# Attention's and the scan's pools each split in two, and a group statistic copied out of its PSUM bank, in a one-layer hybrid encoder step

## The chip, the core and the metric

The kernel runs on one core of one Trainium2 chip. The metric is the device time of one execution in microseconds (us), lower is better. The core has TensorE (matrix products), VectorE, ScalarE, GpSimd and SyncE (SP); here SP issues all the transfers between the device memory and the on-chip memory (SBUF). TensorE writes its results to PSUM, which has eight banks of 2 KB for each of 128 partitions.

## The reference

One layer of an encoder is run over a prompt of 1024 rows and a sample of 64 rows that has a past. Cut to what matters:

```python
xn = _rmsnorm(x, p['norm_mix_w'])
z, xbc, dt_raw, q, k, v, gate_ssm, gate_att = jnp.split(xn @ p['w_in'], ...)
xbc_c, conv_new = _causal_dwconv(conv_past, xbc, ...)          # width 4, then silu
xs, bm, cm = jnp.split(jax.nn.silu(xbc_c), ...)
y_ssm, ssm_new = _ssd_scan(xs, dt, a_neg, bm, cm, ssm_past, chunk_len)
y_ssm = (y_ssm + p['ssm_d'] * xs) * jax.nn.silu(z)
y_ssm = _rmsnorm(y_ssm.reshape(b, t, G, -1), p['ssm_norm_w'])  # over each of 4 groups of 512
o = _diff_attention(rope(rmsnorm(q)), k_all, v_all, q_pos, k_pos, lam)   # softmax pair, a0 - lam * a1
o = _rmsnorm(o, p['subln_w']) * (1.0 - lambda_init)
mix = sigmoid(gate_ssm) * (y_ssm @ p['w_branch_ssm']) + sigmoid(gate_att) * (o @ p['w_branch_attn'])
x = x + mix @ p['w_out']
ha, hb = jnp.split(_rmsnorm(x, p['norm_ffn_w']) @ p['w_up'], 2, axis=-1)
x = x + (jax.nn.silu(_causal_dwconv(ffn_past, ha, ...)) * hb) @ p['w_down']
```

The outputs are x for the prompt and the sample, the keys and values, the scan's states and the last rows of both convolutions.

## The kernel before

Prompt and sample lie side by side as 1088 columns, features on the partitions. The columns are cut in three parts of 384, 384 and 320 (`WIDE`). Each product in float32 is made of three matmuls with operands split in a high and a low half (`product`, L144 to L149); `weights` (L129 to L142) loads a weight block to `w_f` (L139), and ScalarE and VectorE split it (`w_hi` L140, `w_lo` L141).

The work runs in stages:

- Norm, then the v, q and k projections, with rope; the rows go to scratch in the device memory (`q_st`, `k_st`, `c_st`).
- Attention, 8 heads of 9 row blocks. `head_tiles` loads one head's q, k and v; `attend` makes the scores into `sc` (L545, L546), the maximum and exp (L550 or L554, L559), transposes the probabilities into `pt` (L574) and multiplies with v into `po` (L593); `head_out` normalises and stores the head's output (L614 to L621, with the halves `oh` and `ol`).
- The scan, 4 groups by 9 chunks, so 36 steps in 12 spans of `WIDE`. `fetch` loads a span's rows (`in`, `zin`; L654, L656), two spans ahead. `front` makes a step's decay factors from `bc` (L664, L668, L681, L683), transposes x into the bank `tr` (L671) and B into the bank `cb` (L673), copies `cb` out (L676) and forms `xx` (L680). `back` makes the outputs `yi` (L692) and `ye` (L698), and the new state (`stp`, L704 to L711). `gated` multiplies with z and squares; `normed` sums the squares over the group by a matmul with ones into a tile `gst` (L728) that has the tag, and so the bank, of `cb`, takes the inverse root with `rstd_of` (Ln L209, Exp L210, Square L211, two VectorE instructions L212 and L213), scales y (L732) and stores it to `y_sc` (L733).
- The output product, the norm and the feed-forward part.

Between the steps of attention and of the scan, `fill` takes steps of a `filler` on TensorE: the projections of x, z and the gates (`conv_tiles`, `z_tiles`, `gate_tiles`), and later in the scan the first two branch products (`branch`). A filler's result goes to a bank of the pool `pm` (tag `mm`), or, in the scan, to one more bank of the scan's PSUM pool (tag `mx`, through `more` and `acc`).

The order of the instructions on each engine is planned before the run by a scheduler that simulates the times and works by priorities; each engine then runs its own queue in order and waits on semaphores. Memory is handed out in pools. A pool that is opened after another was closed may lie at the same place, and what is written to it waits for the users of the old one. Before the change, attention has one pool in SBUF (`at`) and one in PSUM (`psa`: `sc` with two buffers of two banks, `pt` and `po` with two banks), and the scan has one in SBUF (`sp`) and one in PSUM (`pss`: `tr`, `cb`, `mx`, `yi`, `ye`, `stp`):

```python
    with tc.tile_pool(name="at", bufs=1) as at, tc.tile_pool(name="psa", bufs=1, space=PSUM) as pa:
    ...
    with tc.tile_pool(name="sp", bufs=1) as sp, tc.tile_pool(name="pss", bufs=1, space=PSUM) as pss:
        more = pss, 1
```

Of the kernel before, what the change touches and what calls it, by code (L numbers as in the profile page):

```python
# [17 lines left out]
P = 128  # L18
# [56 lines left out]
def hybrid_layer(ctx: ExitStack, tc: tile.TileContext, xT, prm, cst, rope, wvd, win, wbs, wba, wout, wup, wdn,  # L75
# [409 lines left out]
    with tc.tile_pool(name="at", bufs=1) as at, tc.tile_pool(name="psa", bufs=1, space=PSUM) as pa:  # L485
        lam = at.tile([P, 4], F32, name="lam")
        lt = at.tile([P, 512], F32, name="lt", tag="a_t", bufs=AT)[:, :64]
        wsub = at.tile([P, P], F32, name="wsub")
        V.tensor_scalar_mul(wsub, par[:, O_SUB : O_SUB + P], 1.0 - LAMBDA_INIT)
        for i in range(2):  # L490
            a = O_LAM + 128 * i
            V.tensor_tensor(out=lt, in0=par[:, a : a + 64], in1=par[:, a + 64 : a + 128], op=ALU.mult)
            V.reduce_sum(lam[:, i : i + 1], lt, axis=AX.X)
            act(lam[:, i : i + 1], lam[:, i : i + 1], AF.Exp)
        nlam = at.tile([P, 1], F32, name="nlam")
        V.tensor_tensor(out=nlam, in0=lam[:, 1:2], in1=lam[:, 0:1], op=ALU.subtract)
        V.tensor_scalar_add(nlam, nlam, -LAMBDA_INIT)

        def head_tiles(h):
            def fetch(name, n, b, parts):  # L500
                t = at.tile([P, n], R32, name=name, tag=name, bufs=b)
                for lo, src in parts:
                    load(out=t[lo : lo + src.shape[0]].bitcast(F32), in_=src)
                return t
# [15 lines left out]
        def attend(h, i, tiles, o_t, ssq, s0):  # L520
# [7 lines left out]
            for c in range(2):  # L528
                if nk <= 512:
                    if both is None:  # L530
                        both = pa.tile([P, 1024], F32, name="sc", tag="sc", bufs=2)
# [90 lines left out]

        late = []
        for h in range(8):
            tiles = head_tiles(h)
# [21 lines left out]
    with tc.tile_pool(name="sp", bufs=1) as sp, tc.tile_pool(name="pss", bufs=1, space=PSUM) as pss:  # L647
        more = pss, 1
        def fetch(g, c, w):
            t = sp.tile([P, 6, 384], F32, name="in", tag="in", bufs=2)  # L650
            z = sp.tile([P, 4, 384], F32, name="zin", tag="zin", bufs=2)[:, :, :w]
# [7 lines left out]
        def front(g, ch, o, bx, xs):  # L659
# [3 lines left out]
            bc = sp.tile([P, 8, P], F32, name="bc", tag="bc", bufs=4)  # L663
# [346 lines left out]
```

## Time and profile before

| what | value |
|---|---|
| times of the runs shown, us | 2562.01, 2568.95, 6360.79 |
| their median, us | 2568.95 |
| the profiled execution's own time, us | 2564.99 |
| its span, first to last instruction, us | 2563.2 |
| TensorE busy, us | 2519.5 (98%) |
| VectorE busy, us | 1375.9 (54%) |
| ScalarE busy, us | 1070.6 (42%) |
| GpSimd busy, us | 294.9 (12%) |
| granted TensorE clock, mean | 0.996 |
| bytes moved | 340.42 MB, 133 GB/s in the mean |

Times inside the trace are counted from the span's start. A line of the timeline gives the start, the duration, the engine, the line of the kernel, the operation, out<-in, the shapes and, in brackets, how long the engine had been idle before it and what ended that. SPq is SP's queue: its rows are the issue of transfers, not their duration. `xN` after a row means that N instructions were put together. A wait that has several causes is put down to the one that came last. Matmuls are pipelined, so the busy times of single ones overlap.

### The profile page before, as it was taken

Reading aid. Unit: us, or ns where it says so; the run is one execution under the profiler, and the core shown is the slowest. Engines: PE = TensorE matmul, PEld = TensorE weight load, DVE = VectorE, ACT = ScalarE, POOL = GpSimd, SP = SyncE. Lnnn points to the kernel's source line nnn. Section 1 sums busy time; section 2 is a strip of 40 time slices with the busy share of each in tenths; the row PEclk is TensorE's granted clock in tenths of the full one; section 3 lists DMA queues with packets and bytes.
Section 4 is the critical chain, followed back from the end, with each engine's and each line's share of the span. In section 5 each row is a group of like instructions: output and inputs, shape, how many; then the busy total and the mean of one; then the engine's idle time right before and its main releaser. Section 6 shows DMA issues by size and latency. Waiting matters only on the chain.

```text
span 2563.2 us, 40795 instructions
## 1 busy us (share of the span) xinstructions
PE 2519.5 (98%) x15924; PEld 2436.5 (95%) x15924; DVE 1375.9 (54%) x2359; ACT 1070.6 (42%) x2271; POOL 294.9 (12%) x393
## 2 busy tenths in 40 slices
PE   8999999999999999989999999999999999999999
PEld 8999998999999999988989898999999999999999
DVE  6326265855877577447567657657333333333333
ACT  6234243654666455357455654245313122221221
POOL 3000000100111010014333231022000000000000
PEclk9999999999999999999999999999999999999999
DMA  5218167555445344256796646665311111111112
GB/s 163 82 54 289 47 249 207 164 139 153 119 132 161 112 128 133 68 186 203 219 329 187 226 154 192 193 194 186 120 42 50 42 50 42 43 49 40 44 44 77
DMA packets 216353, 340.42 MB, mean 133 GB/s; under 512 B 28224, under 2 KB 164672, under 8 KB 216032
## 3 DMA queue, kind: packets, MB, share of 16 engines
q1 hardware_dynamic: 216160, 337.81, 42.2%
q8 instruction: 125, 2.05, 0.3%
q14 instruction: 68, 0.56, 0.1%
HBM read 237.60 MB, written 100.13 MB: 132 GB/s over the span
## 4 chain that ended last, share of the span: by engine, by line
PE 86%; DMA 5%; DVE 3%; ACT 3%; SPq 1%; issue 1%; POOL 0%; DVEq 0%; ACTq 0%
PE mm L147 15%; PE mm L149 15%; PE mm L148 15%; PE up L149 7%; PE up L147 7%; PE up L148 7%; PE mx L147 3%; PE mx L149 3%; PE mx L148 3%; PE po L593 3%; PE sc L546 1%; PE sc L545 1%; PE pt L574 1%; DMA b_f<-y_sc 1%; DMA kl_t<-k_st 1%
## 5 line engine op out<-in xcount | busy, mean ns | idle before, releaser
L147 PE MATMUL mm<-xn_hi,w_hi 128*128 128x384 f32 (+1 forms) x1416 | 471.5, 333 | 0.9 <-DVE zr L429 0.9
L149 PE MATMUL mm<-xn_hi,w_lo 128*128 128x384 f32 (+1 forms) x1416 | 468.9, 331 | 0.4 <-DVE w_lo L141 0.4
L148 PE MATMUL mm<-xn_lo,w_hi 128*128 128x384 f32 (+1 forms) x1416 | 467.5, 330 | 0.0
L141 DVE TENSOR_TENSOR w_lo<-w_f,w_hi 128x1024 fp32r<-128x1024 f32 (+2 forms) x196 | 243.5, 1243 | 293.7 <-ACT w_hi L140 293.2
L140 ACT CAST w_hi<-w_f 128x1024 fp32r<-128x1024 f32 (+2 forms) x196 | 203.8, 1041 | 442.8 <-PE mm L148 281.4
L147 PE MATMUL up<-x_hi,w_hi 128*128 128x384 f32 (+1 forms) x1056 | 344.4, 326 | 0.0
L148 PE MATMUL up<-x_lo,w_hi 128*128 128x384 f32 (+1 forms) x1056 | 344.2, 326 | 0.0
L149 PE MATMUL up<-x_hi,w_lo 128*128 128x384 f32 (+1 forms) x1056 | 343.1, 326 | 0.0
L147 PEld LDWEIGHTS mm<-xn_hi,w_hi 128*128 128x128 f32 x1416 | 266.7, 188 | 6.3 <-issue 1.9
L149 PEld LDWEIGHTS mm<-xn_hi,w_lo 128*128 128x128 f32 x1416 | 266.7, 188 | 3.3 <-issue 1.2
L148 PEld LDWEIGHTS mm<-xn_lo,w_hi 128*128 128x128 f32 x1416 | 266.8, 188 | 2.3 <-issue 1.1
L147 PEld LDWEIGHTS up<-x_hi,w_hi 128*128 128x128 f32 x1056 | 198.2, 188 | 0.1
L148 PEld LDWEIGHTS up<-x_lo,w_hi 128*128 128x128 f32 x1056 | 198.2, 188 | 0.0
L149 PEld LDWEIGHTS up<-x_hi,w_lo 128*128 128x128 f32 x1056 | 198.1, 188 | 0.1
L898 DVE TENSOR_TENSOR xa<-xa,mm 128x384 f32<-128x384 f32 x144 | 76.5, 531 | 197.3 <-PE mm L149 197.3
L148 PE MATMUL mm<-f_lo,w_hi 128*128 128x384 f32 (+1 forms) x528 | 173.1, 328 | 0.0
L147 PE MATMUL mm<-f_hi,w_hi 128*128 128x384 f32 (+1 forms) x528 | 173.0, 328 | 0.0
L149 PE MATMUL mm<-f_hi,w_lo 128*128 128x384 f32 (+1 forms) x528 | 173.0, 328 | 0.0
L147 PE MATMUL mm<-b_hi,w_hi 128*128 128x384 f32 (+1 forms) x448 | 149.7, 334 | 3.0 <-DVE b_g L191 2.1
L149 PE MATMUL mm<-b_hi,w_lo 128*128 128x384 f32 (+1 forms) x448 | 146.8, 328 | 2.0 <-DVE w_lo L141 2.0
L148 PE MATMUL mm<-b_lo,w_hi 128*128 128x384 f32 (+1 forms) x448 | 146.6, 327 | 0.0
L458 DVE SCALAR_TENSOR_TENSOR cc<-pre,par,cc 128x384 f32<-128x384 f32 (+1 forms) x216 | 126.5, 586 | 26.0 <-ACT cc L456 20.9
(270 smaller groups left out, 5074.4 us busy)
## 6 DMA issues: line engine op xcount, KB each, us to landing
w_f<-in_win_dram SPq DMA_DIRECT2D x76, 512.0 KB, 4.0
w_f<-in_wup_dram SPq DMA_DIRECT2D x44, 512.0 KB, 3.6
bc<-a_sc SPq DMA_DIRECT2D x32, 512.0 KB, 5.6
w_f<-in_wout_dram SPq DMA_DIRECT2D x24, 512.0 KB, 3.6
x_sc<-cc SPq DMA_DIRECT2D x48, 192.0 KB, 2.0
kh_t<-k_st SPq DMA_DIRECT2D x32, 272.0 KB, 8.4
kl_t<-k_st SPq DMA_DIRECT2D x32, 272.0 KB, 7.8
w_f<-in_wbs_dram SPq DMA_DIRECT2D x16, 512.0 KB, 4.6
```

What stands on the lines that cost most here:

```text
L140: S.copy(hi, w)
L141: V.tensor_tensor(out=lo, in0=w, in1=hi, op=ALU.subtract)
L147: PE.matmul(ps, a_hi, b_hi, start=i == 0, stop=False)
L148: PE.matmul(ps, a_hi, b_lo, start=False, stop=False)
L149: PE.matmul(ps, a_lo, b_hi, start=False, stop=i == n - 1)
L458: V.scalar_tensor_tensor(cc[:, :m], pre[:, i : i + m], cw(i), cc[:, :m], ALU.mult, ALU.add)
L545: PE.matmul(ps[:n, a : a + b], lhs, r_hi, start=True, stop=False)
L546: PE.matmul(ps[:n, a : a + b], lhs, r_lo, start=False, stop=True)
L574: PE.transpose(pt[:kw, (b - b0) * P : (b - b0) * P + n], pr[1][:n, b * P : b * P + kw], ident[:n, :n])
L593: PE.matmul(po[:n, :P], a_t[b // 4][:kw, b % 4 * P : b % 4 * P + n], rhs, start=b == 0, stop=b == nb - 1)
L898: V.tensor_tensor(out=xa[:, m, c : c + w], in0=xa[:, m, c : c + w], in1=ps, op=ALU.add)
```

## The change

- Attention's SBUF pool becomes two: `ak`, opened first, with the tiles of `head_tiles` (q, k, v and the caches), and `at` with the rest. Its PSUM pool becomes `psc` (the `sc` tiles, four banks) and `psa` (`pt`, `po`, two banks).
- The scan's SBUF pool becomes `sin`, opened first, with `in`, `zin` and `bc`, and `sp` with the rest. Its PSUM pool becomes `psi` (`tr`, `cb`, `yi`, `gst` and the fillers' `mx`, four banks) and `pss` (`ye`, `stp`).
- The first head's `head_tiles` is called ahead of the instructions that set up lambda.
- `normed` copies the group sums from `gst` to `rs` in SBUF on ScalarE, and `rstd_of` reads them there.

```diff
-    with tc.tile_pool(name="at", bufs=1) as at, tc.tile_pool(name="psa", bufs=1, space=PSUM) as pa:
-        lam = at.tile([P, 4], F32, name="lam")
...
+    with (tc.tile_pool(name="ak", bufs=1) as ak, tc.tile_pool(name="at", bufs=1) as at,
+          tc.tile_pool(name="psc", bufs=1, space=PSUM) as psc, tc.tile_pool(name="psa", bufs=1, space=PSUM) as pa):
         def head_tiles(h):
             def fetch(name, n, b, parts):
-                t = at.tile([P, n], R32, name=name, tag=name, bufs=b)
+                t = ak.tile([P, n], R32, name=name, tag=name, bufs=b)
...
-            v_t = at.tile([P, 9, P], F32, name="v_t", tag="v_t", bufs=2)
+            v_t = ak.tile([P, 9, P], F32, name="v_t", tag="v_t", bufs=2)
...
-            cv_t = at.tile([P, 4, P], F32, name="cv_t", tag="cv_t", bufs=1)
+            cv_t = ak.tile([P, 4, P], F32, name="cv_t", tag="cv_t", bufs=1)
...
-                    ps = pa.tile([P, 1024], F32, name="sc", tag="sc", bufs=2)
+                    ps = psc.tile([P, 1024], F32, name="sc", tag="sc", bufs=2)
...
+        tiles = head_tiles(0)
+        lam = at.tile([P, 4], F32, name="lam")
...
         for h in range(8):
-            tiles = head_tiles(h)
+            if h:
+                tiles = head_tiles(h)
...
-    with tc.tile_pool(name="sp", bufs=1) as sp, tc.tile_pool(name="pss", bufs=1, space=PSUM) as pss:
-        more = pss, 1
+    with (tc.tile_pool(name="sin", bufs=1) as sin, tc.tile_pool(name="sp", bufs=1) as sp,
+          tc.tile_pool(name="psi", bufs=1, space=PSUM) as psi, tc.tile_pool(name="pss", bufs=1, space=PSUM) as pss):
+        more = psi, 1
         def fetch(g, c, w):
-            t = sp.tile([P, 6, 384], F32, name="in", tag="in", bufs=2)
-            z = sp.tile([P, 4, 384], F32, name="zin", tag="zin", bufs=2)[:, :, :w]
+            t = sin.tile([P, 6, 384], F32, name="in", tag="in", bufs=2)
+            z = sin.tile([P, 4, 384], F32, name="zin", tag="zin", bufs=2)[:, :, :w]
...
-            bc = sp.tile([P, 8, P], F32, name="bc", tag="bc", bufs=4)
+            bc = sin.tile([P, 8, P], F32, name="bc", tag="bc", bufs=4)
...
-            tr = pss.tile([P, 512], F32, name="tr", tag="tr")
+            tr = psi.tile([P, 512], F32, name="tr", tag="tr")
...
-            cb = pss.tile([P, 512], F32, name="cb", tag="cb")
+            cb = psi.tile([P, 512], F32, name="cb", tag="cb")
...
-            yi = pss.tile([P, 4, P], F32, name="yi", tag="yi")
+            yi = psi.tile([P, 4, P], F32, name="yi", tag="yi")
...
-            ps = pss.tile([P, 512], F32, name="gst", tag="cb")[:, :w]
+            ps = psi.tile([P, 512], F32, name="gst", tag="cb")[:, :w]
             PE.matmul(ps, ones, zt[:, 0], start=True, stop=True)
             rs = sp.tile([P, 384], F32, name="grs", tag="grs", bufs=2)[:, :w]
-            rstd_of(sp, rs, ps, w, "gn", 0.25 / 512)
+            S.copy(rs, ps)
+            rstd_of(sp, rs, rs, w, "gn", 0.25 / 512)
```

More of the change, by code (lines that the diff above doesn't have):

```diff
@@ L621, in head_out @@
                     load(out=o_sc[D * u + P * h : D * u + P * (h + 1), b0 * P : b0 * P + w], in_=t.bitcast(F32))
+        tiles = head_tiles(0)
+        lam = at.tile([P, 4], F32, name="lam")
+        lt = at.tile([P, 512], F32, name="lt", tag="a_t", bufs=AT)[:, :64]
+        wsub = at.tile([P, P], F32, name="wsub")
+        V.tensor_scalar_mul(wsub, par[:, O_SUB : O_SUB + P], 1.0 - LAMBDA_INIT)
+        for i in range(2):
+            a = O_LAM + 128 * i
+            V.tensor_tensor(out=lt, in0=par[:, a : a + 64], in1=par[:, a + 64 : a + 128], op=ALU.mult)
+            V.reduce_sum(lam[:, i : i + 1], lt, axis=AX.X)
+            act(lam[:, i : i + 1], lam[:, i : i + 1], AF.Exp)
+        nlam = at.tile([P, 1], F32, name="nlam")
+        V.tensor_tensor(out=nlam, in0=lam[:, 1:2], in1=lam[:, 0:1], op=ALU.subtract)
+        V.tensor_scalar_add(nlam, nlam, -LAMBDA_INIT)
         late = []
         for h in range(8):
-            tiles = head_tiles(h)
+            if h:
+                tiles = head_tiles(h)
             o_t = at.tile([P, 9, P], F32, name="o_t", tag="o_t", bufs=2)
```

13 lines of the change are left out of this document (1 added, 12 removed).

## The prediction

> **What bounds the kernel now.** I read the head of the page first, then the busy time by stages, then the waits of TensorE alone in the scan's stage, and last the order of time round each wait.
>
> ```profile
> PE 2519.5 (98%) x15924; PEld 2436.5 (95%) x15924; DVE 1375.9 (54%) x2359; ACT 1070.6 (42%) x2271; POOL 294.9 (12%) x393
> ```
>
> ```profile
> 0.00:396.00 396.00, 386.48 (x2523) 378.09 (x2524) 181.91 (x308) 155.54 (x319) 23.99 (x37) 1.00 0.44 150
> 396.00:1104.00 708.00, 701.39 (x4484) 674.28 (x4482) 469.89 (x1023) 374.66 (x941) 49.70 (x143) 1.00 0.47 135
> 1104.00:1604.00 500.00, 478.29 (x3157) 433.76 (x3156) 318.96 (x413) 281.37 (x611) 159.44 (x104) 0.98 0.68 216
> 1604.00:2563.20 959.20, 953.34 (x5765) 950.35 (x5764) 405.12 (x617) 259.02 (x401) 61.81 (x109) 1.00 0.26 81
> ```
>
> The columns of the second view are the stretch, its length, the busy time of TensorE, weight load, VectorE, ScalarE and GpSimd, the granted clock, the DMA share and GB/s. TensorE is busy 2519.5 of 2563.2 us, and the change takes no matmul away. So all it can win is idle time (43.7 us in this count) and time at a lowered clock. The third row is the scan: 500.00 − 478.29 = 21.7 us idle, half of the whole, and the only stage whose clock is below 1.00. Attention (second row) idles 6.6 us. The waits of TensorE inside the scan's stage are these:
>
> ```profile
> PE cb L673 <- DVE gn L212: 7.9, 3, 4.7
> PE tr L671 <- DMA in<-x_sc: 4.8, 2, 4.1
> PE mm L147 <- DVE b_g L191: 2.1, 1, 2.1
> PE mx L147 <- DVE ol L619: 1.5, 1, 1.5
> ```
>
> Each row gives us in total, times, longest. Rows one, two and four are what this change is aimed at. The clock falls in the short stretches that hold the longest waits:
>
> ```profile
> 1114.00:1122.00 8.00, 6.21 (x30) 6.18 (x31) 1.75 (x3) 0.37 (x1) 0.00 (x0) 0.79 1.06 375
> 1442.00:1456.00 14.00, 12.61 (x53) 10.67 (x54) 12.92 (x22) 8.72 (x23) 5.38 (x2) 0.63 0.68 214
> 1588.00:1596.00 8.00, 5.94 (x26) 5.70 (x25) 6.44 (x13) 1.34 (x3) 0.00 (x0) 0.79 0.55 182
> ```
>
> At 0.79 over 8 us, 0.21 × 8 = 1.7 us of clock are lost; at 0.63 over 14 us, 0.37 × 14 = 5.2 us.
>
> **Part 1, the boundary from attention to the scan.**
>
> ```profile
> 1091.14 1.05 PE L593 MATMUL po<-v_t,a_t 128*128 128x128 f32 x8
> 1100.45 0.33 SPq L139 DMA_DIRECT2D w_f<-in_win_dram  x1
> 1106.55 0.32 SPq L621 DMA_DIRECT2D o_sc<-ol  x1
> 1106.58 0.44 PE L147 MATMUL mx<-xn_hi,w_hi 128*128 128x384 f32 x1 [1.52 <-DVE ol L619]
> 1108.21 0.80 SPq L654 DMA_DIRECT2D in<-x_sc  x2
> 1109.05 6.70 DMA in<-x_sc
> 1110.90 1.05 ACT L140 CAST w_hi<-w_f 128x1024 fp32r<-128x1024 f32 x1 [5.06 <-PE mx L148]
> 1113.00 0.56 SPq L656 DMA_DIRECT2D zin<-z_sc  x1
> 1115.79 0.90 PE L671 MATMUL tr<-con,in 128*128 128x128 f32 x4 [4.14 <-DMA in<-x_sc]
> ```
>
> The scan's first load (L654) is issued only after the last store of attention's output (L621) has gone, and the filler's bank `mx` opens only when VectorE has read the last `pt` bank (L619). Those are the last users of attention's pools, though `in` and `mx` need only their own place: I read it as one wait for the whole old pool. With two pools, `in`, `zin` and `bc` lie over the q, k and v tiles, whose last reader is the `po` matmul that ends at 1092.2. The four `psi` banks lie over the `sc` banks. The loads can then go some 14 us earlier (to about 1094), land after 6.7 us at about 1101, and be there when TensorE now idles at 1105 and 1111. Removed: 1.52 + 4.14 = 5.7 us, and the 1.7 us of clock behind them: 7.4 us at most, 0 at least if the loads don't move.
>
> What follows next? `e2`, `b_cb` and `xx` stay in a pool that overlaps the end of attention's memory, so ScalarE's and VectorE's part of the first step still waits for about 1108. The first steps also show two short waits (the last row here is a transfer's: how often, KB, us to landing):
>
> ```profile
> 1137.65 0.44 PE L147 MATMUL mx<-xn_hi,w_hi 128*128 128x384 f32 x1 [0.80 <-DVE zr L429]
> 1163.64 0.63 PE L671 MATMUL tr<-con,in 128*128 128x128 f32 x4 [0.66 <-DMA in<-x_sc]
> ...
> w_f<-in_win_dram SPq DMA_DIRECT2D x76, 512.0 KB, 4.0
> ```
>
> I keep their sum, 1.5 us, as the price of an early start whose other operands are not ready. On SP the fetches are issued between 1108.21 and 1113.56, 5.4 us; moved ahead, they stand before the weight load of 1100.45 (landing 4.0 us after issue) and the output stores. 1100.45 + 5.4 + 4.0 = 1109.9, and its cast starts at 1110.90: covered by 1 us, and up to 5.4 us late if the fetch also crowds the engines, whose share is 1.06 in the first stretch above. I take 0 of that and keep 5.4 for the range. **Boundary: −7.4 + 1.5 = −5.9 us** (from −7.4 to +5.4).
>
> **Part 2, the statistics copied out of their bank.**
>
> ```profile
> 1199.38 1.28 ACT L209 ACT_TABLE_LOAD   x1
> 1205.60 0.33 PE L673 MATMUL cb<-con,in 128*128 128x128 f32 x1 [1.25 <-DVE gn L212]
> 1278.92 1.28 ACT L209 ACT_TABLE_LOAD   x1
> 1283.84 0.33 PE L673 MATMUL cb<-con,in 128*128 128x128 f32 x1 [1.88 <-DVE gn L212]
> 1424.64 0.88 PE L728 MATMUL gst<-zin,con 128*128 128x384 f32 x2 [0.47 <-ACT b_cb L676]
> 1435.43 1.28 ACT L209 ACT_TABLE_LOAD   x1
> 1442.79 0.55 DVE L212 SCALAR_TENSOR_TENSOR gn<-gst,gn 128x384 f32<-128x384 f32 x1
> 1443.39 0.33 PE L673 MATMUL cb<-con,in 128*128 128x128 f32 x1 [4.74 <-DVE gn L212]
> ```
>
> `gst` shares the one `cb` bank with the transposes of the next step, and holds it until L212 has read it, behind Ln with a table load, Exp, and Square on ScalarE. A copy at the place of the first table load frees the bank instead. Its price is the nearest row of like shape:
>
> ```profile
> L187 ACT COPY b_g<-mm 128x384 f32<-128x384 f32 (+1 forms) x16 | 7.1, 443 | 9.5 <-PE mm L149 9.5
> ```
>
> With 0.44 us the bank is free at 1199.8, 1279.4 and 1435.9. TensorE came to it at 1205.60 − 1.25 = 1204.35, at 1281.96 and at 1438.65: no wait is left, by 4.5, 2.6 and 2.8 us. Removed: 7.9 us. The clock's 5.2 us at 1442 to 1456 follow the longest of them and should go too. **Bank: −13.1 us** (from −13.1 to −7.9 if the clock falls all the same).
>
> The Trainium skill, "TensorE: Matmul & The Clock Gate", section "Part 1: The HAM clock gate (the warmup mystery)", has the clock halved after an idle window of about 3.4 us. By that rule the waits of 4.14 and 4.74 us trip it and the short ones do not, so all 6.9 us return; the rows differ in one place, since the clock also fell at 1588, after a wait of 2.06 us, so a short leftover could keep part of it.
>
> The copies themselves: 12 × 0.443 = 5.3 us on ScalarE, which is busy 281 of 500 us in the stage. They lengthen each normalisation by 0.44 us. That is hidden by filler matmuls, except where the chain ends on TensorE:
>
> ```profile
> 1582.30 1.28 ACT L209 ACT_TABLE_LOAD   x1
> 1587.85 1.94 DVE L732 SCALAR_TENSOR_TENSOR y<-y,par,grs 128x320 f32<-128x320 f32 x4
> 1590.31 0.54 PE L147 MATMUL mm<-b_hi,w_hi 128*128 128x384 f32 x1 [2.06 <-DVE b_g L191]
> ```
>
> Here b_g L191 stands behind L732 on VectorE and TensorE waits for it. I charge this place and one more (the y rows that the first branch over y_sc loads): **+0.9 us**, from 0.4 to 5.3.
>
> The Trainium skill, "VectorE: DVE Perf Modes", section "Rules for kernel authors", speaks against the copy: take operands from PSUM as they are, or copy first only for many operations. Here two readers follow, so by that rule the copies are 5.3 us lost and the sum would be 4.4 us higher, 2551. The sum above goes by the waits on the bank instead: what the copy buys is the bank and not a faster read.
>
> **Part 3, the first head's loads ahead of the lambda set-up, and attention's two pools.** TensorE's first scores wait for a load of k, not for the set-up:
>
> ```profile
> 396.42 1.51 SPq L503 DMA_DIRECT2D q_t<-q_st  x3
> 399.11 0.15 DVE L497 TENSOR_SCALAR nlam<-nlam 128x1 f32<-128x1 f32 x1
> 414.81 0.47 PE L546 MATMUL sc<-kl_t,q_t 128*128 128x512 f32 x1 [1.14 <-DMA kl_t<-k_st]
> ```
>
> The set-up ends at 399.1, 15 us before the scores run, and both halves of the memory still follow the same q/k stage. 0 us; at most 1.1 either way.
>
> **The sum.** The profiled execution took 2564.99 us around a span of 2563.2. It lies between the two closest of the runs shown, 2562.01 and 2568.95 (their median). 2565.0 − 5.9 − 13.1 + 0.9 = **2546.9 us**, 0.7% under the profiled execution and 0.9% under the median. Best case: 2565.0 − 7.4 − 13.1 + 0.4 = 2544.9, and runs lie up to 3 us under the profiled one: 2542. With a leftover clock dip and the copies exposed the forecast's own range is 2542 to 2556.
>
> **Rivals.**
>
> *The gain is given back at the scan's end.* From 1563 to 1590 the chain of waits runs over loads of y_sc, ScalarE and VectorE, with TensorE idle in small pieces. If that chain doesn't move up, TensorE reaches it earlier and waits longer. Then part 2 is lost and the boundary stays: 2565.0 − 5.9 + 0.9 = 2560. For it: the 2.1 us row. Against it: TensorE paces the 36 scan steps through matmuls in one queue, so the chain should come earlier with them.
>
> *The split does not do what it says:* the loads are held by something else, such as SP's queue. Part 1 is 0: 2565.0 − 13.1 + 0.9 = 2553. Against it: L654 goes out 1.7 us after the last L621.
>
> *Slower: the freed bank draws the next transposes ahead of ScalarE.* The order on TensorE is planned beforehand. If the planner takes the copy as done at once, it puts the `cb` transposes straight behind `gst`, ahead of filler matmuls, and TensorE stands until ScalarE, in order, reaches the copy. That ScalarE is late shows at 1424.64 + 0.88 = 1425.5 against 1435.43. At the mean of the three waits, 7.9 / 3 = 2.6 us, plus 0.44, at all 12 places: 36.5 us for the 7.9 there now, and no clock regained: 2565.0 − 5.9 − 7.9 + 36.5 = 2588. It decides once the 12 together pass 7.9 + 5.2 + 5.9 = 19 us, 1.6 us each. Spread to all 36 steps that use this bank it is 36 × 3.04 = 109 us and 2661. Against both: fillers have stood between in all but three cases.
>
> **Chances.** Forecast 0.52; given back 0.17; split idle 0.10; slower at the 12 places 0.12; slower at all steps, or another loss of that size, 0.07; something faster by over 2% 0.02, since 2% is 51 us and only 43.7 us of idle time and the 8.6 us of clock in the three rows above are there to be won. Faster and slower by over 2%, about what a measurement of this kernel can tell from no change, have 0.02 and 0.07; the rest, 0.91, is within 2%. The range reaches from 2541 (one us under the best case) to the slower rival at 2588.
>
> **What would show it.** Right: the first L654 is issued before 1097, no `tr` wait of 4 us, no `mx` wait on L619; no wait of `cb` on L212, 12 new ScalarE copies of about 0.44 us; the clock 1.00 round the eighth `gst`; scan stage near 482 us. Wrong: L654 still behind the last L621; a wait of `cb` on the new copy of over 1.6 us in the mean; the wait on b_g L191, or those on y_sc loads, grown by 10 us; TensorE's busy time changed by more than 5 us, which would mean that the order changed elsewhere.

## The result and the profile after

| kernel | median us (runs) | ratio to before, 95% interval |
|---|---|---|
| before | 2565.36 (2561.38 to 2569.66, and one of 6360.79; 10 runs) | 1 |
| changed | 2558.16 (2555.86 to 2559.6, 10 runs) | 0.9972 [0.9963, 0.9981] |

The change gains 7.2 us, 0.28%; the ratio leaves out the one execution of 6360.79 us. The forecast was 2546.9, so 11 us of the gain are missing. The profiled execution of the changed kernel took 2559.57 us around a span of 2557.7.

The first row of the changed kernel's page with the busy times, and then its windows by stage (columns as in the prediction): the scan's stage first, then four shorter stretches:

```profile
PE 2521.8 (99%) x15924; PEld 2439.8 (95%) x15924; DVE 1378.1 (54%) x2359; ACT 1074.6 (42%) x2283; POOL 292.8 (11%) x393
```

```profile
1104.00:1604.00 500.00, 483.76 (x3175) 439.18 (x3174) 325.11 (x419) 286.09 (x624) 159.29 (x104) 0.98 0.67 212
...
1194.00:1206.00 12.00, 11.29 (x37) 9.33 (x38) 4.04 (x8) 9.00 (x20) 1.09 (x1) 0.57 0.62 190
1428.00:1458.00 30.00, 26.79 (x157) 23.47 (x158) 19.74 (x30) 23.70 (x57) 8.62 (x5) 0.89 0.78 247
1566.00:1596.00 30.00, 26.48 (x138) 25.77 (x138) 17.83 (x33) 13.15 (x23) 3.29 (x2) 0.89 0.75 244
...
1090.00:1190.00 100.00, 98.65 (x682) 89.74 (x681) 59.04 (x82) 63.52 (x148) 35.86 (x25) 1.00 0.63 204
```

The twelve copies show as ScalarE's 2283 instructions for 2271. TensorE has the same work and 500.00 − 483.76 = 16.2 us of idle time in the scan, where it had 21.7. The clock did not come back: at 1194 it is 0.57 over 12 us, 5.2 us lost at a place where the kernel before lost none. The rows at 1428 and 1566 lose 0.11 × 30 = 3.3 us each. That is 11.8 us of clock in the scan; the three rows of the prediction have 8.6 for the kernel before.

TensorE's waits in the scan's stage now (total, times, longest, us):

```profile
PE mm L147 <- ACT b_hi L171: 5.3, 3, 2.7
PE cb L677 <- ACT grs L734: 4.3, 2, 2.8
...
PE ye L702 <- DVE y L703: 1.2, 1, 1.2
```

The waits of `tr` on its load and of `mx` on attention's last bank are gone. The wait of `cb` on L212 is gone by name, and a wait of the same instruction on the new copy (L734) stands in its place. New are 5.3 us on the casts of rows of `y_sc` (`b_hi`, L171).

The timeline at the boundary from attention to the scan:

```profile
1089.54 1.05 PE L581 MATMUL po<-v_t,a_t 128*128 128x128 f32 x8
1090.63 0.79 SPq L658 DMA_DIRECT2D in<-x_sc  x2
...
1096.36 10.06 SPq L668 DMA_DIRECT2D bc<-a_sc  x4
...
1098.24 0.27 PE L675 MATMUL tr<-con,in 128*128 128x128 f32 x1
...
1108.47 0.38 SPq L609 DMA_DIRECT2D o_sc<-oh  x1
```

The first load goes out with the end of the last `po` matmul, 17.6 us earlier than before (1108.21), and `tr` runs at 1098 without a wait.

And the timeline at two of the copies, the places of the waits of 1.5 and 2.8 us:

```profile
1187.14 0.81 PE L732 MATMUL gst<-zin,con 128*128 128x384 f32 x2
...
1190.10 4.20 ACT L687 ACTIVATE bc<-bc,nacum 128x128 f32<-128x128 f32 x14
1194.20 0.46 ACT L734 COPY grs<-gst 128x384 f32<-128x384 f32 x1
...
1194.71 0.33 PE L677 MATMUL cb<-con,in 128*128 128x128 f32 x1 [1.53 <-ACT grs L734]
...
1418.26 0.88 PE L732 MATMUL gst<-zin,con 128*128 128x384 f32 x2 [1.30 <-ACT b_cb L680]
...
1426.23 2.44 ACT L687 ACTIVATE bc<-bc,nacum 128x128 f32<-128x128 f32 x8
1428.58 0.45 ACT L734 COPY grs<-gst 128x384 f32<-128x384 f32 x1
...
1429.09 0.33 PE L677 MATMUL cb<-con,in 128*128 128x128 f32 x1 [2.76 <-ACT grs L734]
```

`gst` is done at 1187.95 and at 1419.14; the copies start 6.2 and 9.4 us later, because other work stands ahead of them in ScalarE's queue. TensorE has come to `cb` by then, and earlier than it would without the copies. The fillers are counted by the matmuls into `mm` and `mx`: in the two traces, 19 to 24 filler matmuls stand between a `gst` and the next `cb` at the first ten places, and 24 to 48 with the pools alone (e3 below; 22 and 48 behind the eighth, at 1418).

### The profile page after: what moved, and what is told of

It is laid out like the page before. It is cut to its first block, busy times and chain, and to the rows that moved or that the text cites. A ratio compares the mean times of both kernels' runs of the same rounds, so it can differ in the third digit from the quotient of the medians.

```text
span 2557.7 us, 40802 instructions
## 1 busy us (share of the span) xinstructions
PE 2521.8 (99%) x15924; PEld 2439.8 (95%) x15924; DVE 1378.1 (54%) x2359; ACT 1074.6 (42%) x2283; POOL 292.8 (11%) x393
## 4 chain that ended last, share of the span: by engine, by line
PE 71%; DMA 4%; ACT 3%; DVE 3%; issue 1%; SPq 0%; POOL 0%; DVEq 0%; ACTq 0%; POOLq 0%
PE mm L147 13%; PE mm L149 13%; PE mm L148 12%; PE up L149 7%; PE up L147 7%; PE up L148 7%; PE po L581 3%; DMA b_f<-y_sc 1%; PE sc L534 1%; PE sc L533 1%; PE pt L562 1%; PE mx L149 1%; PE mx L147 1%; PE mx L148 1%; PE yi L696 1%
```

## The experiments

Each kernel was timed in five rounds beside the kernel before on the same chip, those of one letter together. Medians in us; across letters the ratios are compared, a difference of 0.001 being 2.6 us.

| run | what it is | us | ratio to before |
|---|---|---|---|
| e1 | the changed kernel again | 2558.42 | 0.9971 [0.9959, 0.9982] |
| e2 | copies only | 2565.53 | 0.9996 [0.9985, 1.0006] |
| e3 | pools only | 2552.94 | 0.9948 [0.9935, 0.9961] |
| e4 | both, copies on VectorE | 2556.85 | 0.9962 [0.9948, 0.9976] |
| f1 | PSUM pools only | 2554.42 | 0.9950 [0.9938, 0.9962] |
| f2 | SBUF pools only | 2569.44 | 1.0014 [1.0005, 1.0023] |
| f3 | both, bank still held | 2559.45 | 0.9971 [0.9961, 0.9982] |
| f4 | pools, `gst` in the bank of `stp`, no copy | 2562.96 | 0.9991 [0.9982, 0.9999] |
| g1 | changed, one cast moved off ScalarE | 2563.18 | 0.9987 [0.9978, 0.9997] |
| g2 | pools, copy in the last normalisation only | 2557.15 | 0.9956 [0.9942, 0.9969] |
| g3 | pools, copies not in the last group | 2556.94 | 0.9959 [0.9945, 0.9973] |
| g4 | pools, copy in the eighth normalisation only | 2553.21 | 0.9945 [0.9930, 0.9960] |
| h1 | pools, copies off every chain | 2554.91 | 0.9957 [0.9945, 0.9970] |
| h2 | pools, last chain longer | 2555.45 | 0.9962 [0.9948, 0.9975] |
| h3 | pools, fewer fillers in the scan | 2541.47 | 0.9908 [0.9894, 0.9921] |
| i1 | before, fewer fillers | 2563.01 | 0.9994 [0.9985, 1.0003] |
| i2 | changed, fewer fillers | 2556.32 | 0.9968 [0.9957, 0.9980] |
| i3 | pools, still fewer fillers | 2563.45 | 0.9995 [0.9985, 1.0005] |

Most intervals are 0.0025 wide, some 6 us, so two kernels of the table that lie 3 us apart are not told apart by it.

### Which part of the change does what (e1 to e4)

e1 has no edit. e2 is the kernel before with the copy, e3 the changed kernel without it, e4 the copy on another engine:

```diff
 e2, on before:
+            S.copy(rs, ps)
-            rstd_of(sp, rs, ps, w, "gn", 0.25 / 512)
+            rstd_of(sp, rs, rs, w, "gn", 0.25 / 512)
 e3, on the changed kernel:
-            S.copy(rs, ps)
-            rstd_of(sp, rs, rs, w, "gn", 0.25 / 512)
+            rstd_of(sp, rs, ps, w, "gn", 0.25 / 512)
 e4, on the changed kernel:
-            S.copy(rs, ps)
+            V.tensor_copy(rs, ps)
```

> The changed kernel as it is, once more. Its first profile shows TensorE at half clock five times in the scan (10.24 us from 1195, then 3.4 us at 1430, 1454, 1567 and 1591: 23.9 us, 11.9 us lost; before: 17.1 us, 8.5 us lost). Theory 'the dips belong to the program': the same five dips within a few us, mean clock 0.995 to 0.996, 2558 us. Rival 'the dips fall by chance, as the clock's windows happen to lie to the waits': the waits of TensorE are the same within 1 us, but dips come at other places or with other lengths, and mean clock and time move together by 2 to 5 us.

> The kernel before with the copy of the group sums alone; all pools as before. The forecast's theory (the bank is free 0.44 us after the place of the table load): no wait of cb on the statistics, clock not below 1.00 round the eighth group sum, 12 us faster than before, 2553 us. Rival 'ScalarE is late, and the plan puts the copy behind the exps of bc': the copy starts 5 to 10 us after its matmul at two or three of the twelve places, cb still waits 3 to 5 us in all where it waited 7.9, and the gain is 2 to 5 us, 2560 to 2563 us.

> The changed kernel without the copy: the pools alone. The forecast's theory: no wait at the boundary on attention's last store, 6 us faster than before, 2559 us, and cb still waits about 8 us on L212. Rival 'the boundary's gain is spent in the next 100 us (new waits and a clock dip at 1195)': the boundary's waits are gone, but only 2 to 4 us are left at the scan's end, 2561 to 2563 us. If the two parts simply add, this run and the copy alone together are 7.2 us faster than before.

> The changed kernel with the copy on VectorE in place of ScalarE. Theory 'ScalarE's queue makes the copy late': VectorE is free or nearly so at both places where cb waits on the copy (group sums at 1187 and 1418), so the copy ends within 2.5 us of the matmul, the 4.3 us of waits on it go, and with them a clock dip of 1.7 to 5.1 us: 3 to 9 us faster than the changed kernel, 2549 to 2555 us. Rival 'what is freed at the bank is lost elsewhere (loads of y_sc, the next wait)': the waits on the copy go, others grow, and the time stays within 2 us of 2558; the twelve copies of 0.53 us on VectorE cost up to 6 us more.

The pools alone win 13.1 us. The copies alone win nothing, and on top of the pools they cost 5.5 us (e3 to e1, 2558.42 − 2552.94). So the missing 11 us all lie with the copies, and the pools bring more than forecast (e3 is faster than both of its expectations). The two parts do not add: alone they gain 13.1 and 0.5 us, together 7.6 (e1, on the same chip).

In e1's trace the clock falls at the same five places as in the first trace of this kernel, the first time for 6.8 us instead of 10.2, and its ten executions reach from 2552.1 to 2562.0. So the places recur and the lengths vary, and each of its two expectations is right in a part. e2 has neither of its times: `cb` still waits 3.0 us, on the copy, as the rival said, but next to nothing is gained. With the copies on VectorE (e4) the kernel is not told apart from either; the waits on the copy are gone and others have come up (`gst` 3.3 us on the copy of `b_cb`, `ye` 2.1 us), as e4's rival has it.

TensorE's waits in the scan with the pools alone:

```profile
PE cb L677 <- DVE gn L212: 6.3, 3, 4.9
PE yi L696 <- DVE bc L688: 2.5, 1, 2.5
PE mm L147 <- DVE b_g L191: 1.8, 1, 1.8
```

The bank's waits are still there (6.3 us), and no cast of `y_sc` is waited for. The copies trade 6.3 us on L212 for 4.3 on L734 and 5.3 on L171.

### Which pool is the lock (f1, f2)

f1 takes the split of the SBUF pools back, f2 that of the PSUM pools; neither has a copy.

```diff
 f1:
-    with (tc.tile_pool(name="sin", bufs=1) as sin, tc.tile_pool(name="sp", bufs=1) as sp,
+    with (tc.tile_pool(name="sp", bufs=1) as sp,
 f2:
-          tc.tile_pool(name="psi", bufs=1, space=PSUM) as psi, tc.tile_pool(name="pss", bufs=1, space=PSUM) as pss):
-        more = psi, 1
+          tc.tile_pool(name="pss", bufs=1, space=PSUM) as pss):
+        more = pss, 1
```

> Only the PSUM pools are split (psc/psa, psi/pss); memory stays one pool each, and there is no copy. Theory (the boundary is paid by two locks, memory and banks, each with its own price): the wait of mx on L619 (1.5 us before) goes, the wait of tr on the load of in stays at 4 us or a little more, because L654's load still follows the last store L621; time 1 to 3 us under before, about 2564 where before is 2566. Rival (the locks act only together, the later one sets the end): no change within 1 us, 2566. Rival (banks are the main lock): 9 us or more under before, about 2556.

> Only the memory pools are split (ak/at, sin/sp); PSUM stays one pool each, and there is no copy. Theory (two locks): the loads of the first scan step are issued some 14 us earlier than before and the 4.1 us wait of tr on them goes; mx and tr still open only when VectorE has read the last pt bank (L619 of before), so a wait of about 1.5 us stays; with the clock of that place 5 to 7 us under before, about 2560. Rival (the locks act only together): no change, 2566. Rival (memory is all of it): 13 us under before, 2553, like both splits together.

For f1 the rival with the banks as the main lock holds; f2 lies above all three of its expected times. The window from 1090 to 1190 in the kernel before, in f1 and in f2:

```profile
1090.00:1190.00 100.00, 91.92 (x617) 83.31 (x616) 57.33 (x78) 59.22 (x139) 33.63 (x22) 0.98 0.62 196
```

```profile
1090.00:1190.00 100.00, 97.56 (x675) 88.88 (x675) 58.23 (x79) 60.86 (x144) 32.84 (x24) 1.00 0.64 202
```

```profile
1090.00:1190.00 100.00, 85.20 (x577) 77.63 (x576) 55.82 (x76) 58.20 (x137) 31.87 (x21) 0.93 0.60 191
```

In the same 100 us TensorE runs 617, 675 and 577 matmuls. In f1 the first load is issued as late as before:

```profile
1108.78 0.80 SPq L658 DMA_DIRECT2D in<-x_sc  x2
```

Yet TensorE idles for only 2.4 us in its window, since the fillers' bank `mx` is free and the plan puts more fillers between the last `po` and the first `tr`, 131 instead of 97. In f2 the loads are early and it goes worse; its timeline:

```profile
1089.93 1.53 SPq L658 DMA_DIRECT2D in<-x_sc  x2
...
1095.48 10.24 SPq L668 DMA_DIRECT2D bc<-a_sc  x4
...
1107.79 0.88 SPq L609 DMA_DIRECT2D o_sc<-oh  x2
...
1114.15 0.23 DVE L607 TENSOR_TENSOR ol<-pt,oh 128x64 fp32r<-128x64 f32 x1 [14.41 <-DMA o_sc<-oh]
...
1114.43 1.11 PE L675 MATMUL tr<-con,in 128*128 128x128 f32 x4 [11.65 <-DVE ol L607]
```

The `bc` loads stand in SP's queue for 10 us, attention's last stores wait behind them, L606 and L607 wait for the stores, and `tr` waits 11.65 us, since the scan's one bank pool opens only when attention's last `pt` bank has been read. In the changed kernel the stores are as late (1108.47, above), but `tr` no longer needs those banks. So the SBUF split is harmful by itself. Whether it adds anything to the PSUM split (e3 under f1 by 1.5 us) is not told.

### Why the copies cost: the bank, the time or the order (f3, f4, g1)

f3 makes the copies but reads on from the bank, so that it stays held. f4 makes none and puts `gst` in another bank. g1 is the changed kernel with one cast of L171 per branch on GpSimd.

```diff
 f3, on the changed kernel (the copy is read by nobody):
-            rstd_of(sp, rs, rs, w, "gn", 0.25 / 512)
+            rstd_of(sp, rs, ps, w, "gn", 0.25 / 512)
 f4, on e3:
-            ps = psi.tile([P, 512], F32, name="gst", tag="cb")[:, :w]
+            ps = pss.tile([P, 512], F32, name="gst", tag="stp")[:, :w]
 g1, on the changed kernel:
-                    S.copy(hi[:, k], t)
+                    (G.tensor_copy if (c, k) == (768, 3) else S.copy)(hi[:, k], t)
```

> Both pool splits, and the twelve ScalarE copies are made, but L212 goes on reading the bank, which therefore stays held; the copied tile is read by nobody. Theory 1 (the copies lose on top of the pools because they free the bank, and the order on TensorE then takes the cb transposes ahead of fillers and stands behind a late ScalarE): the loss goes with the freed bank, time within 1.5 us of the 2552.9 of the pools alone. Theory 2 (the copies' own 12 x 0.44 us on ScalarE, in front of casts that TensorE waits for, are the loss): 5 us above the pools alone, about 2558, as in the changed kernel, with the waits of mm on b_hi at the end of the scan.

> Both pool splits and no copy; the statistics gst stand in the bank of stp instead of cb, so that the cb transposes never wait for the normalisation, and the next stp (which comes 3 to 20 matmuls after the transposes) does. Theory 1 (what is lost is the early order behind a late ScalarE, not the ScalarE time of a copy): the 4.9 us wait of cb on L212 goes, but stp, later in its step, waits in its place for the same reader, shorter by the work between: 0 to 4 us under the pools alone, 2549 to 2553. Theory 2 (only the ScalarE time of the copies hurt, and a free cb bank is worth its whole 6.3 us of waits and the clock behind): 9 us or more under the pools alone, 2544 or less.

> The changed kernel, in which one y_sc cast of each of the two branches that read y_sc (column block 768, row block 3; L171) is made on GpSimd instead of ScalarE. The orders on TensorE and VectorE are the changed kernel's; on ScalarE the last copy L734 then stands behind three casts, as the last Ln does with the pools alone, and not behind a fourth one that waits for its y_sc load until 1575.7. Theory 1 (at the scan's end the changed kernel pays for the order on ScalarE, not for the copy): the last normalisation starts about 3 us earlier and the wait of mm on b_hi at 1588 (2.8 us) falls under 1 us; 2.5 to 4 us under the changed kernel, 2554 to 2556. Theory 2 (the copies' own 12 x 0.44 us on the chain): no change, 2558 to 2559.

f3 costs some 6 us over the pools alone (0.9971 to 0.9948) with the bank still held and with 24 to 48 fillers behind a `gst`, as without the copies, so my theory that the freed bank is the harm falls. f4 frees the bank of `cb` with no copy at all and is 11 us slower than the pools alone (0.9991), which neither of its expectations had. Its waits:

```profile
PE stp L708 <- DVE gn L212: 8.7, 6, 2.8
PE cb L677 <- ACT b_cb L680: 5.5, 2, 4.8
PE mm L147 <- ACT b_hi L171: 4.0, 2, 2.5
```

The same reader L212 is waited for, only in another bank, and more in sum; so f4 does not show what a free bank is worth. g1 was to mend ScalarE's order at the scan's end, and both of its expectations missed: it is 4 us slower than the changed kernel (0.9987 to 0.9971 and 0.9972). There the copy no longer stands behind the cast but behind TensorE itself:

```profile
1578.87 0.43 ACT L734 COPY grs<-gst 128x320 f32<-128x320 f32 x1 [2.63 <-PE gst L732]
```

So at the scan's end the last `gst` is late on TensorE. (Where g1's own 4 us lie is not shown: from the last `stp` to the first `mix` matmul it takes 114.4 us, the changed kernel 114.6.) In the planned orders 90 filler matmuls stand between the last `stp` and it wherever every normalisation has a ScalarE copy (the changed kernel, e2, f3, g1), and 74 in the kernel before, e3, e4, f1 and g2 to g4; f4, without a copy, has 96. At 0.15 to 0.17 us each, the distance of fillers' starts in the timeline, 16 are 2.4 to 2.8 us. In the traces the last `gst` starts 19.0 us after the end of the last `stp` in the changed kernel and 14.6 in e3.

### One copy at a time (g2 to g4)

```diff
 on e3, with the condition (g, c) == (3, 768) for g2, g < 3 for g3, (g, c) == (2, 384) for g4:
-            rstd_of(sp, rs, ps, w, "gn", 0.25 / 512)
+            src = ps
+            if <condition>:
+                S.copy(rs, ps)
+                src = rs
+            rstd_of(sp, rs, src, w, "gn", 0.25 / 512)
```

> Both pool splits, and the copy in the last of the twelve normalisations only; in this kernel's order it stands behind three casts, as the last Ln does with the pools alone. Theory 1 (order, not copy): the chain at the scan's end is longer by the copy's 0.44 us at most; 2553 to 2554, within 1 us of the pools alone (2552.9). Theory 2 (a copy on this chain is what costs the 3 us at the scan's end): 2556 or more.

> Both pool splits, and the copy in the nine normalisations of the first three groups, not in the last group's three; the order on ScalarE at the scan's end is that of the pools alone (three casts ahead of the last Ln). Theory 1: the 3 to 5 us that the changed kernel loses after 1550 are not there, what it loses at 1180 to 1205 (about 4 us) and gains at 1427 to 1454 (about 2 us) stays: 2554 to 2556. Theory 2 (each copy costs about the same, 5.5 us over twelve): 2557 to 2558.

> Both pool splits, and the copy in one normalisation only, the eighth, where cb waits 4.9 us for L212 with the pools alone and the clock is halved for 13.7 us behind it (6.8 us lost). If a copy in time frees the bank there, up to 11.7 us are to be had; the copy stands on ScalarE behind the first eight L687 and y_sc casts, as in the changed kernel, where cb still waited 2.8 us there. Theory 1 (the bank is free only when ScalarE gets to the copy): 2 to 6 us under the pools alone, 2547 to 2551, with a cb wait on the copy of 1 to 3 us and a half-clock stretch of 3.4 us. Rival (the bank is what holds TensorE, and one copy frees it): 9 us or more, 2544 or less. Rival (the wait only moves to another operand that ScalarE makes): 2552 or more.

g2, one copy in the last normalisation, is 2 us over the pools alone by the ratio (0.9956 to 0.9948) and 4 by the median: it goes with the theory that a copy on this chain costs, and its trace says the same (below). g3, with the nine copies of the first three groups, lies between its two expectations, 3 us over the pools alone, and its interval takes in both. g4 stands level with e3, as the last of its three expectations has it. In its trace `cb` waits 3.1 us at 1427 instead of 4.9, and then two casts of L171 are waited for, 1.8 us, with a dip of the clock of their own: the rival in which the wait moves to another product of ScalarE.

### Time, or length of the last chain (h1, h2)

```diff
 h1, on e3:
+            S.copy(rs, con[:, :w])
             rstd_of(sp, rs, ps, w, "gn", 0.25 / 512)
 h2, on e3 (copies read by nobody):
+            for _ in range(6 if (g, c) == (3, 768) else 0):
+                S.copy(rs, ps)
             rstd_of(sp, rs, ps, w, "gn", 0.25 / 512)
```

> Both pool splits; in each of the twelve normalisations ScalarE copies a constant tile into grs ahead of its use (0.42 to 0.47 us each, the same size as the changed kernel's copies). The copy needs no result of gst, so it lies on no chain, frees no bank, and the order at the scan's end is that of the pools alone (74 filler matmuls ahead of the last gst). Theory 1 (the copies cost by standing between gst and Ln, on the chain to the y_sc casts): within 2 us of the pools alone, 2551 to 2555, and no new wait of mm on b_hi over 1.5 us after 1560. Theory 2 (12 x 0.44 us more ScalarE work is the cost, wherever it stands): 5 us over the pools alone, 2558.

> Both pool splits; in the last normalisation alone ScalarE copies gst six times into a tile that is not read, ahead of Ln, so that this one chain is about 2.5 us longer; the bank stays held and the order on TensorE ahead of the last gst is that of the pools alone (74 fillers). Theory 1 (the y_sc round trip behind the last normalisation sets the scan's end, with next to no slack): from the last stp to the y_sc casts 34 us instead of 31.4, from the last stp to the first mix matmul 113 to 114 us instead of 110.7, a wait of mm on b_hi of 2 to 4 us near 1585; time 2 to 4 us over the pools alone, 2555 to 2557. Theory 2 (that chain has cover): the 2.5 us lie beside fillers, no wait on b_hi grows, 2552 to 2553.5.

h1 has the copies' ScalarE time without their place on a chain. It is 2 us over e3, within the intervals of both, and its scan ends as with the pools alone, so the theory that twelve copies' time is the price wherever they stand gets less than half of its 5 us. h2 lengthens one chain. By tile, the last `stp` and the first matmuls of the output product (a row gives the count, the shortest, middle and longest ns, the first and last start) in e3, in the changed kernel and in h2:

```profile
L708 PE MATMUL stp<-xx,b_cb x2: 589/641/693, 1553.1 to 1553.6; 64*128 64x512 f32 x2
...
L147 PE MATMUL mm<-mix,w_hi x30: 336/336/338, 1664.8 to 1680.0; 128*128 128x384 f32 x30
```

```profile
L708 PE MATMUL stp<-xx,b_cb x2: 589/641/693, 1555.1 to 1555.6; 64*128 64x512 f32 x2
...
L147 PE MATMUL mm<-mix,w_hi x19: 336/336/368, 1670.2 to 1679.6; 128*128 128x384 f32 x19
```

```profile
L708 PE MATMUL stp<-xx,b_cb x2: 589/641/693, 1551.2 to 1551.7; 64*128 64x512 f32 x2
...
L147 PE MATMUL mm<-mix,w_hi x26: 336/336/416, 1666.4 to 1679.6; 128*128 128x384 f32 x26
```

And the timelines of the same three, ScalarE's first casts of `y_sc` rows that follow the last normalisation, in h2 with the matmul that waits for them:

```profile
1585.56 1.35 ACT L171 CAST b_hi<-b_f 128x320 fp32r<-128x320 f32 x3 [1.77 <-DMA b_f<-y_sc]
```

```profile
1590.75 0.88 ACT L171 CAST b_hi<-b_f 128x320 fp32r<-128x320 f32 x2 [1.24 <-DMA b_f<-y_sc]
```

```profile
1586.80 0.89 ACT L171 CAST b_hi<-b_f 128x320 fp32r<-128x320 f32 x2 [1.22 <-DMA b_f<-y_sc]
...
1587.31 0.56 PE L147 MATMUL mm<-b_hi,w_hi 128*128 128x320 f32 x2 [2.72 <-ACT b_hi L171]
```

From the last start of `stp` to the first `mix` matmul it is 111.2 us in e3, 114.6 in the changed kernel and 114.7 in h2; and to the casts 32.0, 35.1 and 35.1. (Taken from the end of `stp`, 110.2 to 111.2 us in the kernel before, e3, f1, f2, g3, g4 and h1, whose last normalisation has no copy; 113.1 to 115.4 in the changed kernel, e1, e2, e4, f3, g1, g2 and h2, which all have copies in it; and 117.3 in f4, which has none, but 96 fillers ahead of the last `gst`.) The store and load of `y_sc` behind the last normalisation set the scan's end with next to no slack, and h2's 2.5 us come back as 3.5. Of the copies' 5.5 us, 3.4 lie here. The later `gst` (19.0 us behind `stp` instead of 14.6) is enough for it. What a copy costs here by itself is less clear: g2's single copy takes 0.42 us, and its stretch is 2.5 us longer than e3's (113.7 instead of 111.2), of which I cannot place 2.

### With more fillers left for the scan's end (h3, i1 to i3)

```diff
-SCAN_STEPS = 1.65
+SCAN_STEPS = 1.5     # h3 on e3, i1 on before, i2 on the changed kernel; 1.4 for i3 on e3
```

> Both pool splits without the copies, and fewer filler matmuls in the scan (SCAN_STEPS 1.5 instead of 1.65), so that more of them are left to lie beside the y_sc round trip at its end. If the waits at the scan's end (1.1 and 1.8 us and a half-clock stretch of 3.4 us with the pools alone) are a lack of filler there, they go: 2 to 4 us under the pools alone, 2549 to 2551. If the scan's own steps need the fillers as cover, waits of yi and cb inside the scan grow by more than that: 2555 or more.

> The kernel before, with SCAN_STEPS 1.5 instead of 1.65 and nothing else; no split, no copy. If the gain of fewer fillers in the scan (11 us on top of the pools) and that of the pools (13 us) are separate, this stands 10 to 12 us under before, 2553 to 2556. If the fewer fillers only pay because the pools moved the boundary, within 3 us of before, 2562 to 2568.

> The changed kernel with SCAN_STEPS 1.5 instead of 1.65: both splits and the twelve copies. Theory 1 (with 1.65 the copies cost because they make the y_sc round trip at the scan's end later, where no filler covers it): with the round trip covered by the fillers that are left over, the copies cost nothing or gain the cb waits that are left with the pools at this setting (4.4 us): 2537 to 2543, against 2541.5 without the copies. Theory 2 (the copies cost inside the scan, through the order that they give TensorE and ScalarE): 4 us or more above it, 2545.5 or more.

> Both pool splits without the copies, SCAN_STEPS 1.4: one more step in the direction that won 11 us. If filler at the scan's end is still short at 1.5, 2 us or more faster, 2539.5 or less; at 1.5 no wait of over 0.9 us is left after 1445, so I expect nothing there and more waits in the scan's steps for want of cover: 2541 to 2547.

h3 beats both kernels: 24 us under before, 10 under the pools alone (0.9908 to 0.9948). The same setting does nothing without the split (i1), and with the copies it brings 1 us, which is not told from nothing (i2, 0.9968 to 0.9972). At 1.4 all is lost again (i3), so 1.5 is one order that fits and no trend; neither h3 nor i3 came out at one of its expected times. i3's executions reach from 2553.0 to 2566.5 us with granted clocks from 0.997 down to 0.993, and the one with the trace is the fastest, so the trace does not show its loss. TensorE's waits in the scan in h3, and its window from 1424 to 1470:

```profile
PE cb L677 <- DVE gn L212: 4.4, 2, 3.3
PE yi L696 <- DVE bc L688: 3.9, 2, 2.4
```

```profile
1424.00:1470.00 46.00, 42.60 (x285) 38.17 (x284) 35.24 (x46) 28.48 (x65) 16.34 (x10) 0.96 0.77 242
```

At 0.96 over 46 us, 1.8 us of clock are lost. With the pools alone at 1.65 it is 0.34 × 20 = 6.8 us at this place, and 1.8 more in the window from 1566 to 1596 (0.94), where h3 stands at 1.00:

```profile
1426.00:1446.00 20.00, 15.09 (x68) 12.74 (x67) 12.41 (x24) 13.74 (x36) 6.24 (x2) 0.66 0.71 219
```

So over half of what the rate brings is clock: some 7 us of the 10 to 11.

The same of i2, with the copies:

```profile
PE mm L147 <- ACT b_hi L171: 3.2, 1, 3.2
PE mm L148 <- DVE b_lo L172: 2.8, 1, 2.8
PE yi L696 <- ACT y L706: 2.6, 1, 2.6
PE mx L147 <- ACT w_hi L140: 2.5, 1, 2.5
...
PE cb L677 <- ACT grs L734: 1.7, 2, 1.6
```

```profile
1424.00:1470.00 46.00, 36.55 (x206) 32.19 (x205) 32.99 (x45) 28.69 (x65) 13.63 (x10) 0.89 0.66 207
```

The copies do what they are for, 4.4 us of waits for the bank fall to 1.7, and TensorE waits instead for casts, copies and weights that the same ScalarE makes, or VectorE right behind it (`b_lo`): 206 matmuls in 46 us instead of 285. This falls inside the scan and not at its end, so at this rate my theory that the loss is the end's alone falls.

### Where the time lies, in two stretches

The scan can be cut at three matmuls: the end of the last `po`, the last start of `stp`, and the first matmul with `mix`. In the kernel before the first is at 1092.19 (in the prediction) and the second at 1564.3; in e3 they are at 1090.00 and 1553.6 (above):

```profile
L704 PE MATMUL stp<-xx,b_cb x4: 589/594/693, 1552.2 to 1564.3; 128*128 128x512 f32 x2, 64*128 64x512 f32 x2
```

```profile
1088.95 1.05 PE L581 MATMUL po<-v_t,a_t 128*128 128x128 f32 x8
```

| trace | last `po` to last `stp`, us | last `stp` to first `mix`, us |
|---|---|---|
| before | 472.1 | 111.3 |
| e2, copies only | 465.4 | 116.0 |
| e3, pools only | 463.6 | 111.2 |
| changed | 465.0 | 114.6 |
| e1, changed again | 463.1 | 115.0 |
| h3, pools at 1.5 | 429.1 | 134.1 |
| i2, changed at 1.5 | 441.8 | 136.9 |

Each row is one execution, and the two of the changed kernel differ by 1.9 us in the first stretch. There the pools gain 8.5 us and the copies alone 6.7, but both together only 7.1 and 9.0: the two gains overlap, and on top of the pools the copies bring nothing. In the second stretch every row with copies is longer: by 3.4 to 4.7 us at 1.65, by 2.8 at 1.5. At 1.5 the copies cost 12.7 us in the first stretch as well.

## Why the prediction was wrong

**Part 1, the boundary: right in what goes, wrong in why, and too small.** The signs named came true: the first load before 1097, no wait of `tr` and of `mx`. The step that failed is "The loads can then go some 14 us earlier ... and be there when TensorE now idles". The earlier loads alone bring nothing (f2); the four banks bring it (f1). The size, −5.9, was too small by the 1.5 us that I kept for two short waits, which did not stay: from 1090 to 1190 TensorE was idle for 100 − 91.92 = 8.1 us before, for 2.5 us in e3 and for 1.35 us in the changed kernel. That is 5.6 to 6.7 us, and with the 1.7 us of clock 7.3 to 8.4. The traces agree: 8.5 us up to the last `stp`. The pools' times measure 13.1. Of the rest the two traces show 2.2 us ahead of the last `po` (1092.2 to 1090.0), 1.7 of it a fall of the clock near 437 us that of the two only the trace of the kernel before has; and the two profiled executions lie some 2 us nearer together than the medians. The 5.4 us that I kept for loads ahead of the stores in SP's queue were real: they are f2's mechanism, at 11.65 us. In the changed kernel the stores are as late, and TensorE does not wait for them.

**Part 2, the copies: wrong.** The forecast was −13.1 for the bank and +0.9 for the copies; on top of the pools they measure +5.5. The first failed step is "A copy at the place of the first table load frees the bank ... no wait is left". I held TensorE's order fixed; the plan made it anew and put `cb` up to 26 fillers nearer to `gst`, while the copies started 6.2 and 9.4 us after it, and 4.3 us of 7.9 stayed. That ScalarE is late stood in the slower rival with its row, and the sum did not use it. The second is "Removed: 7.9 us" as a gain on top of part 1: in g4, e4 and i2 a wait taken from the bank comes back as a wait for what ScalarE and VectorE make next, and the gains of the two parts overlap. Of the bank's −13.1 on top of the boundary nothing was had: from the last `po` to the last `stp` the copies add 1.4 us to e3 in one execution and take 0.5 in the other (e1). The third is the clock, "should go too": it fell at 1194 behind waits of 1.2 and 1.5 us, and the scan lost 11.8 us to it instead of 8.6. The copies' price of 0.9 left out the chain at the scan's end, which costs 3.4 us. The sign that I named for a changed order, TensorE's busy time, did not show it: it moved by 2.3 us while the fillers between `gst` and `cb` went from between 24 and 54 to between 19 and 24.

The Trainium skill, "VectorE: DVE Perf Modes", section "Rules for kernel authors", advises to copy out of PSUM first only for many operations. The trace agrees in the sign (e3 against e1, 5.5 us), though the runs show another reason than the copies' time: in h1 that time is not told from nothing.

**Part 3** cost nothing that the traces show.

**The sum.** Part 1 was 13.1 instead of 5.9, the copies +5.5 instead of −12.2: 7.2 us better and 17.7 worse, 2546.9 − 7.2 + 17.7 = 2557.4, against 2558.2.

**The rivals.** "The gain is given back at the scan's end" (2560) came nearest and names the right chain, loads of `y_sc`, ScalarE and VectorE. For the copies alone it fits: e2 gains 6.7 us inside the scan and gives back 4.7 at its end. With the pools it holds for 3.4 us, and there is no gain of the copies to give back; that its 2560 lies so near 2558.2 is in part luck, since two errors offset each other: its boundary was too small (5.9 for 13.1), and so was its price of the copies (0.9 for 5.5). "The freed bank draws the next transposes ahead of ScalarE" is what the plan did, at all of the first ten places, but TensorE stood at two only, 4.3 us in sum, under the 19 us from which it would decide: 19 or more fillers were left between. That the split would do nothing is refuted by e3.

**Open:** why the plan gives up cover with twelve copies that it keeps without them, why the gains of the pools and of the copies overlap, why one filler rate in three fits the pools so well, and where the last 2 us of the copies' 5.5 lie at the rate of 1.65: the two traces of the changed kernel do not show them inside the scan.

## What to carry to other kernels

In this kernel a wait for a shared bank was not worth taking away, because the engine that frees it had no time to spare just there: where ScalarE is behind, a copy is one more thing that it is late with, and the wait moves to its next product. Two gains on one stretch may overlap, so price the second with the first in place. When one pool follows another, look for the split that frees what the waiting engine writes (here the PSUM banks), and ask what an earlier load pushes back in its queue. After a stall is gone, try the rate of the filler work again, for one step of it moved more here than the whole change, and the next step lost it again.

## What the runs showed of the hardware

The granted clock falls behind shorter waits than I had taken it to, and for longer. In the changed kernel it was 0.57 from 1194 to 1206 behind waits of 1.20 us (`ye`, to 1184.95) and 1.53 us (`cb`, to 1194.71). Nor does the length of a wait decide: with the pools alone `yi` waits 2.53 us to 1181.27, and the clock stays at 1.00 from 1176 to 1196. The Trainium skill, "TensorE: Matmul & The Clock Gate", section "Part 1: The HAM clock gate (the warmup mystery)", has an idle window of about 3.4 us before the clock is halved. The rows here do not agree: no single wait near 1194 is half as long.
